# Final LayerNorm of a decoder layer: scaling on ACT and bias by accumulating transfers, last block on VectorE

## Chip, core and metric

The kernel runs on one core of one Trainium2 chip. The metric is device time in microseconds of one execution, the median of several runs; lower is better.

## The reference, cut to what matters

One decoder layer runs over a prompt of 512 rows and over 32 sample rows (8 sequences of 4), 2048 columns wide, in float32. The change lies in its last step, the output product with its residual and the LayerNorm behind it:

```python
def _layernorm(x, w, b):
    xf = x.astype(jnp.float32)
    mu = jnp.mean(xf, axis=-1, keepdims=True)
    var = jnp.mean(jnp.square(xf - mu), axis=-1, keepdims=True)
    return (xf - mu) * lax.rsqrt(var + LN_EPS) * w.astype(jnp.float32) + b.astype(jnp.float32)
...
    out = jnp.einsum('btc,cd->btd', y, w_out)
    return _layernorm(DN_ALPHA * x + out, ln_w, ln_b).astype(x.dtype)
```

The rest of the layer (the input projection, an mLSTM branch, a sliding-window attention branch and their gated merge) is the same before and after.

## The kernel before

The whole program is written out by Python loops. A list scheduler then orders each engine's instructions by a simulated timeline, among the ready ones by their place in the program; `tc.issue_after(x)` holds a block's instructions behind instruction `x` on its engine. Each engine works through its list in order and waits on semaphores. VectorE is DVE in the profile, TensorE is PE, GpSimd is POOL; SP issues the plain transfers, POOL the accumulating ones.

Most of the program is float32 products made of three products of split operands. The output product `y · w_out` runs over 16 column tiles of 128. Tiles 0 to 12 give transposed results: each is copied out of the accumulator by ACT and turned back by TensorE in `add_residual`, where VectorE adds `ALPHA * x`. The sums stand in one buffer, `z`, of 128 partitions by 4 blocks by 2048 columns; block t holds rows 128t to 128t + 127 of the prompt. The 32 sample rows lie folded into `zs`, 128 partitions by 512. `stats` gathers the LayerNorm statistics of each 512 columns as they come. In `residual_task`, `scaled(1, ...)` multiplies block 1 by `ln_w` in advance.

The last three column tiles (`G3 = 3`) are made transposed only for blocks 2 and 3 and the samples. For blocks 0 and 1 `rows_of(0)` and `rows_of(1)` make them as plain rows, the last large products of the program; each of these calls slips other work in behind its second step (`meanwhile`). So the order at the end is: the first two steps of `rows_of(0)`; the last residual of blocks 2, 3 and the samples, their `moments` and their `finish`; the rest of `rows_of(0)`; the first steps of `rows_of(1)`; block 0's residual, moments and `finish`; the rest of `rows_of(1)`; block 1.

`moments` makes mean and variance on VectorE and the power −1/2 on POOL (L1621), into the columns `m` and `r_` of `mv`. `finish` normalises a block in two halves of 1024 columns with two VectorE operations each: `(z - m) * lw` (L1635) and `z * r_ + lb` (L1640), and then stores each half to `y_p`. For the samples (t = 4) they are L1626 and L1627, with `lwq` and `lbq`. Block 0's second operation and its stores are put off (`later=True`, `rest0`) until block 1's statistics are through; `add_rows(1)`, block 1's residual and moments, is held behind block 0's first operations.

Block 1 ends in `finish_last`. As it is already multiplied by `lw`, what is left is `z * r_ + (lb - m * r_ * lw)`. The bracket is made by TensorE: `mr` holds `-m * r_` and a one for each row, is turned into two rows (`mrT`), and a product with the two rows `ln_w`, `ln_b` (`lrows`) gives 512 columns at a time (L1656). VectorE adds (L1657) and SP stores 256 KB (L1658), four times.

Elsewhere in the kernel POOL already issues accumulating transfers, which add one 512 KB buffer to another of the same shape (L617), and ACT already scales by a column of its own for each partition (L762).

Of the kernel before, what the change touches and what calls it, by code (L numbers as in the profile page):

```python
# [15 lines left out]
F32 = mybir.dt.float32  # L16
F32R = mybir.dt.float32r
AF = mybir.ActivationFunctionType
ALU = mybir.AluOpType

D = 2048
# [15 lines left out]
EPS = 1e-5  # L37
# [36 lines left out]
def _build(tc, nc, i, o, es):  # L74
# [3 lines left out]
    def pool(stack, name, bufs, space=None, side=None):  # L78
        kw = {"space": space} if space is not None else {}
        if space is None:  # L80
            kw["side"] = side or "right"
            kw["reuse_waits"] = "tile"
        return stack.enter_context(tc.tile_pool(name=name, bufs=bufs, **kw))

    y_p, y_s, C_p, n_p, m_p, kb_p, vb_p, C_s, n_s, m_s, kb_s, vb_s = o
    V, A, G, PE = nc.vector, nc.scalar, nc.gpsimd, nc.tensor
# [13 lines left out]
    def nm(s):  # L100
        count[0] += 1
        return f"{s}_{count[0]}"

    def sm():
        return psB.tile([128, 512], F32, tag="sm", name=nm("sm"))

    def ev(n=T):
        return evp.tile([128, n], F32, tag="ev", name=nm("ev"))
# [16 lines left out]
    state = {}  # L125
# [10 lines left out]
    def drain():  # L136
        while live:
            tick()
# [4 lines left out]
    ident = cc[:, C_ID:C_ID + 128]  # L143
# [161 lines left out]
    for g in range(8):  # L305
        for q in range(2):
            k = g * 2 + q
            pt = sm()
# [9 lines left out]
            else:  # L318
                hilo(pt[:], xk2[0][k // 4 - 2][:, k % 4, 0:SEQ], xk2[1][k // 4 - 2][:, k % 4, 0:SEQ])
                c = (slice(None), k - 8, slice(0, SEQ - HT))  # L320
                V.tensor_tensor(out=s1r[c], in0=pt[:, HT:SEQ], in1=s1r[c], op=ALU.subtract)
        if g % 2:
# [7 lines left out]
            else:  # L330
                hilo(src, *(xk2[p][g // 2 - 2][:, :, SEQ:T] for p in range(2)))
                c = (slice(None), slice(k4.start - 8, k4.stop - 8), slice(SEQ - HT, HT))
# [930 lines left out]
    def branch(src, p, tmp, ahead=()):  # L1263

        hs, los = act_tiles(p, "bh"), act_tiles(p, "bl")

        def steps():
            for k in range(KT):
                if k < len(ahead):
                    st = ahead[k]  # L1270
                else:
                    st = tmp(k)
                    nc.sync.dma_start(st[:], src[k])
                hilo(st[:], hs[k // 4][:, k % 4], los[k // 4][:, k % 4])
                yield
        return (hs, los), whole(hs), whole(los), steps()

    _, bah, bal, g_ = branch(d_bra, act, lambda k: ev(), ahead)
# [264 lines left out]
    d1 = pool(esD, "d1", 1)  # L1543
    z = d1.tile([128, 4, D], F32, name="z")
    lw = d1.tile([128, D], F32, name="lw")
    lb = d1.tile([128, D], F32, name="lb")
    zs = d1.tile([128, 512], F32, name="zs")[:]
    stt = d1.tile([128, 5, 4, 6], F32, name="stt")
    mv = d1.tile([128, 5, 4], F32, name="mv")
# [7 lines left out]
        nc.sync.dma_start(z[:, :, cs], xrows[:, :, cs])  # L1557
        nc.sync.dma_start(zs[r], xs_src[:, cs])

    mr = d1.tile([128, 2], F32, name="mr")  # L1560
    V.memset(mr[:], 1.0)

    def load_ln():
        nc.sync.dma_start(lw[:], i["ln_w"].partition_broadcast(128))
        nc.sync.dma_start(lb[:], i["ln_b"].partition_broadcast(128))
# [20 lines left out]
    def stats(lo, hi, c4):  # L1586
        for t in range(lo, min(hi, 4)):
            V.bn_stats(stt[:, t, c4], z[:, t, c4 * 512:c4 * 512 + 512])

    def scaled(t, c4):  # L1590
        c = slice(c4 * 512, c4 * 512 + 512)
        V.tensor_tensor(out=z[:, t, c], in0=z[:, t, c], in1=lw[:, c], op=ALU.mult)

    def evac(ot, ps, parts=(0, 1)):
        for f, c, w in CUT:
            if f in parts:
                A.copy(ot[:, c:c + w], ps[f][:, :w])

    def residual_task(ct, ot):
        add_residual(ct, ot, 0, 5)  # L1600
        if ct % 4 == 3:
            yield
            stats(0, 4, ct // 4)
            yield
            scaled(1, ct // 4)

    def moments(t):
        m = mv[:, t]
        if t < 4:
            V.bn_aggr(m[:, 0:2], stt[:, t])  # L1610
            state["moment"] = V.tensor_scalar(m[:, 1:2], m[:, 1:2], EPS, None, op0=ALU.add)
        else:
            V.bn_stats(stt[:, t, 0], zs)
            V.bn_aggr(m[:, 0:2], stt[:, t, 0:1])
            V.scalar_tensor_tensor(m[:, 1:2], m[:, 0:1], m[:, 0:1], m[:, 1:2], op0=ALU.mult, op1=ALU.add)
            pm = sm()
            PE.matmul(pm[:, 0:2], cq, m[:, 0:2], start=True, stop=True)
            V.tensor_copy(m[:, 0:2], pm[:, 0:2])
            V.scalar_tensor_tensor(m[:, 3:4], m[:, 0:1], m[:, 0:1], m[:, 1:2], op0=ALU.mult, op1=ALU.subtract)
            V.tensor_scalar(m[:, 1:2], m[:, 3:4], -1.0, EPS, op0=ALU.mult, op1=ALU.add)  # L1620
        G.tensor_tensor(out=m[:, 2:3], in0=m[:, 1:2], in1=mh[:, 0:1], op=ALU.pow)  # L1621

    def finish(t, later=False):
        m, r_ = mv[:, t, 0:1], mv[:, t, 2:3]
        if t == 4:
            V.scalar_tensor_tensor(zs, zs, m, lwq, op0=ALU.subtract, op1=ALU.mult)  # L1626
            V.scalar_tensor_tensor(zs, zs, r_, lbq, op0=ALU.mult, op1=ALU.add)  # L1627
            for q in range(4):
                nc.sync.dma_start(ys_rows[:, q * 512:q * 512 + 512], zs[q * 32:q * 32 + 32])
            return  # L1630
        dst = y_p[0, t * 128:t * 128 + 128, :]
        cs = [slice(c0, c0 + 1024) for c0 in range(0, D, 1024)]
        for c in cs:
            zt = z[:, t, c]
            state["scaled"] = V.scalar_tensor_tensor(zt, zt, m, lw[:, c], op0=ALU.subtract, op1=ALU.mult)  # L1635

        def rest():
            for c in cs:
                zt = z[:, t, c]
                V.scalar_tensor_tensor(zt, zt, r_, lb[:, c], op0=ALU.mult, op1=ALU.add)  # L1640
                nc.sync.dma_start(dst[:, c], zt)
        if later:
            return rest
        rest()

    def finish_last(t):

        m, r_ = mv[:, t, 0:1], mv[:, t, 2:3]
        V.scalar_tensor_tensor(mr[:, 0:1], m, -1.0, r_, op0=ALU.mult, op1=ALU.mult)
        pt = sm()  # L1650
        PE.transpose(pt[:2, 0:128], mr[:], ident)
        A.copy(mrT, pt[:2, 0:128])
        for q in range(4):
            c = slice(q * 512, q * 512 + 512)
            pc = sm()
            PE.matmul(pc[:], mrT, lrows[q // 2][:2, (q % 2) * 512:(q % 2) * 512 + 512], start=True, stop=True)  # L1656
            V.scalar_tensor_tensor(z[:, t, c], z[:, t, c], r_, pc[:], op0=ALU.mult, op1=ALU.add)  # L1657
            nc.sync.dma_start(y_p[0, t * 128:t * 128 + 128, c], z[:, t, c])  # L1658

    def tail_task(ct, ot):  # L1660
        add_residual(ct, ot, 2, 5)
# [2 lines left out]
    def add_rows(t):  # L1664

        cs = slice(D - G3 * 128, D)
        V.scalar_tensor_tensor(z[:, t, cs], z[:, t, cs], ALPHA, rows[t][:, 0:G3 * 128], op0=ALU.mult, op1=ALU.add)
        stats(t, t + 1, 3)
        moments(t)
# [3 lines left out]
    def rows_of(t, meanwhile):  # L1673
        ps = rows[t] = sm()
        for k in range(KT):
            if k == 2:
                meanwhile()
            yk = slice(t * 128, t * 128 + 128)
            hi, lo = yh_[k // 4][:, k % 4, yk], yl_[k // 4][:, k % 4, yk]
            for n, (a, p) in enumerate(((hi, 0), (hi, 1), (lo, 0))):  # L1680
                PE.matmul(ps[:, 0:G3 * 128], a, w3[k // 8][p][:, k % 8].rearrange("p g c -> p (g c)"),
                          start=(k == 0 and n == 0), stop=(k == KT - 1 and n == 2))
# [14 lines left out]
    for g in range(G3):  # L1697
        ct = 16 - G3 + g
        ps = sm()
        for half in range(2):  # L1700
            raw = load_half(wo, ct * 128, half)
            wh, wl = (w[:, :, g] for w in w3[half])
# [7 lines left out]
    def room(tag):  # L1710
        return wp.tile([128, 8, 128], F32, tag=tag, name=nm("room"))[:].rearrange("p a b -> p (a b)")

    lq, cm = room("wh"), room("wh")
    lwq, lbq, cq, mrT = lq[:, 0:512], lq[:, 512:1024], cm[:, 0:128], cm[:2, 128:256]
    nc.sync.dma_start(cq, i["consts"][:, C_Q:C_Q + 128])
    for q in range(4):
        r, cs = slice(q * 32, q * 32 + 32), slice(q * 512, q * 512 + 512)
        nc.sync.dma_start(lwq[r], i["ln_w"][cs].partition_broadcast(32))
        nc.sync.dma_start(lbq[r], i["ln_b"][cs].partition_broadcast(32))
    lrows = [room("wl") for _ in range(2)]  # L1720
    for h in range(2):
        for n, name in enumerate(("ln_w", "ln_b")):
            nc.sync.dma_start(lrows[h][n:n + 1], i[name][h * 1024:h * 1024 + 1024].unsqueeze(0))
    rows_of(0, lambda: (add_residual(15, ot, 2, 5), stats(2, 4, 3), [moments(t) for t in (2, 3, 4)], finish(2), finish(3), finish(4)))
    rest0 = []
    rows_of(1, lambda: (add_rows(0), rest0.append(finish(0, later=True))))
    with tc.issue_after(state["scaled"].ins):
        add_rows(1)
    with tc.issue_after(state["moment"].ins):
        rest0[0]()  # L1730
        scaled(1, 3)
    finish_last(1)
    drain()
    esD.close()

# [27 lines left out]
```

## Time and profile before

| | us |
|---|---|
| median of 3 runs (2523.73 to 2529.15) | 2525.47 |
| the profiled execution, its time | 2526.54 |
| its span, first to last instruction | 2524.8 |
| mean granted clock of TensorE | 0.994 |

Times in the profile count from the start of the span. Busy time of an engine is the sum of its instructions; a row of the timeline gives start, duration, engine, line, operation, what it writes and reads, the shape, how many were merged, and in brackets the idle time before it and what ended that. A row of the transfers gives packets, megabytes and the time that the packets took as a share of 16 DMA engines over the window asked for. A time to landing is counted from the issue of a transfer.

### The profile page before, as it was taken

How to read it: one execution, taken by the hardware profiler on the slowest of the kernel's cores; microseconds unless marked ns; L12 is line 12 of the kernel's file. 1: busy time of each engine (PE TensorE's matmuls, PEld its weight loads, DVE VectorE, ACT ScalarE, POOL GpSimd, SP SyncE). 2: the span in 40 equal slices, each digit the busy share in tenths (PEclk: the TensorE clock that was granted, in tenths of full speed). 3: DMA queues.
4: the chain of work that ended last, by engine and by line, in shares of the span. 5: the costliest groups of instructions: out<-in, count | busy, mean ns of one | idle time of the engine just before them, and what ended most of it. 6: DMA issues, size and time to landing. Idle time of an engine off the chain costs nothing.

```text
span 2524.8 us, 48516 instructions
## 1 busy us (share of the span) xinstructions
PE 2496.1 (99%) x19667; PEld 2430.7 (96%) x19667; DVE 1765.6 (70%) x2690; ACT 1210.3 (48%) x1966; POOL 364.6 (14%) x347
## 2 busy tenths in 40 slices
PE   8999999999999999999999999999999999999997
PEld 8999999999999999999999999999999999999996
DVE  8867777677677677777777877777856655764335
ACT  4457676676676664443433544434633333433220
POOL 0111211211211211122111222111000000110000
PEclk8999999999999999999999999999999999999998
DMA  6776666666666654577577577576755556888232
GB/s 167 169 188 160 152 151 160 152 149 162 152 148 163 152 143 116 129 219 221 165 226 223 156 215 219 170 225 199 231 176 173 184 170 208 217 218 268 84 108 82
DMA packets 544505, 439.86 MB, mean 174 GB/s; under 512 B 44084, under 2 KB 451556, under 8 KB 543992
## 3 DMA queue, kind: packets, MB, share of 16 engines
q1 hardware_dynamic: 531320, 389.30, 52.1%
q0 software_dynamic: 12960, 47.45, 9.9%
q8 instruction: 154, 2.52, 0.4%
q14 instruction: 71, 0.58, 0.1%
HBM read 305.76 MB, written 90.04 MB: 157 GB/s over the span
## 4 chain that ended last, share of the span: by engine, by line
PE 52%; issue 4%; DVE 1%; DMA 1%; POOL 0%; ACT 0%; POOLq 0%; DVEq 0%
PE bank L639 20%; PE bank L204 12%; PE bank L641 10%; PE sm L1334 2%; PE sm L1153 1%; PE sm L1147 1%; PE sm L1366 1%; PE sm L1379 1%; PE sm L204 1%; DMA tx<-d_brm 1%; PE sm L1656 0%; PE sm L1313 0%; PE sm L1321 0%; PE sm L1575 0%; DVE z L1640 0%
## 5 line engine op out<-in xcount | busy, mean ns | idle before, releaser
L195 ACT CAST wh<-raw 128x1024 fp32r<-128x1024 f32 x620 | 649.2, 1048 | 860.1 <-PE bank L639 620.5
L196 DVE TENSOR_TENSOR wl<-raw,wh 128x1024 fp32r<-128x1024 f32 x620 | 764.1, 1233 | 294.4 <-ACT wh L195 254.3
L639 PE MATMUL bank<-xk,wh 128*128 128x272 f32 x2336 | 321.8, 288 | 0.6 <-DVE ev L664 0.6
L639 PEld LDWEIGHTS bank<-xk,wh 128*128 128x128 f32 x2336 | 303.6, 188 | 4.2 <-ACT wh L195 1.7
L619 DVE TENSOR_TENSOR raw<-raw,raw 128x1024 f32<-128x1024 f32 x230 | 292.2, 1272 | 10.2 <-DMA raw<-in_w_in 5.5
L658 POOL TENSOR_TENSOR ev<-p,ev 128x272 f32<-128x272 f32 x78 | 117.7, 1509 | 570.1 <-ACT ev L657 515.9
L641 PE MATMUL bank<-xk,wl 128*128 128x272 f32 x1168 | 173.5, 288 | 0.0
L639 PE MATMUL bank<-n2h,wh 128*128 128x272 f32 x624 | 160.6, 288 | 2.1 <-ACT wh L195 2.1
L639 PE MATMUL bank<-s1h,wh 128*128 128x272 f32 x624 | 161.9, 290 | 0.7 <-ACT wh L195 0.7
L639 PE MATMUL bank<-n3l,wh 128*128 128x272 f32 x624 | 161.4, 290 | 0.0
L639 PE MATMUL bank<-s4h,wh 128*128 128x272 f32 x624 | 161.1, 289 | 0.1
L639 PE MATMUL bank<-n3h,wh 128*128 128x272 f32 x624 | 161.1, 289 | 0.0
L639 PE MATMUL bank<-n2l,wh 128*128 128x272 f32 x624 | 160.8, 290 | 0.0
L639 PE MATMUL bank<-s1l,wh 128*128 128x272 f32 x624 | 160.7, 290 | 0.0
L639 PE MATMUL bank<-s4l,wh 128*128 128x272 f32 x624 | 160.4, 290 | 0.0
L641 PEld LDWEIGHTS bank<-xk,wl 128*128 128x128 f32 x1168 | 156.7, 188 | 0.1
L639 PE MATMUL bank<-a11l,wh 128*128 128x272 f32 x584 | 150.1, 290 | 0.0
L639 PE MATMUL bank<-a11h,wh 128*128 128x272 f32 x584 | 149.9, 288 | 0.0
L204 PE MATMUL bank<-bh,wl 128*128 128x272 f32 x704 | 148.1, 289 | 0.0
L204 PE MATMUL bank<-bh,wh 128*128 128x272 f32 x704 | 147.8, 290 | 0.0
L204 PE MATMUL bank<-bl,wh 128*128 128x272 f32 x704 | 147.2, 288 | 0.0
L639 PEld LDWEIGHTS bank<-n2h,wh 128*128 128x128 f32 x624 | 117.2, 188 | 2.5 <-ACT wh L195 2.3
(443 smaller groups left out, 5619.0 us busy)
## 6 DMA issues: line engine op xcount, KB each, us to landing
raw<-in_w_in SPq DMA_DIRECT2D x296, 512.0 KB, 4.7
raw<-raw POOLq DMA_DIRECT2D x82, 512.0 KB, 4.9
C<-in_state_mlstm_C SPq DMA_DIRECT2D x32, 1024.0 KB, 6.3
out<-C SPq DMA_DIRECT2D x64, 512.0 KB, 3.8
raw<-in_w_proj_a SPq DMA_DIRECT2D x32, 512.0 KB, 4.8
raw<-in_w_proj_m SPq DMA_DIRECT2D x32, 512.0 KB, 5.5
raw<-in_w_out SPq DMA_DIRECT2D x32, 512.0 KB, 4.1
d_sgm<-ev SPq DMA_DIRECT2D x16, 272.0 KB, 4.1
```

Source lines behind the costliest of these rows:

```text
L195: A.copy(wh[:, k:k + n], raw[:, k:k + n])
L196: V.tensor_tensor(out=wl[:, k:k + n], in0=raw[:, k:k + n], in1=r32(wh[:, k:k + n]), op=ALU.subtract)
L204: PE.matmul(ps[f][:, :w], a[:, kk], b(k, c, w), start=(k == 0 and n == 0), stop=(k == 15 and n == 2))
L619: V.tensor_tensor(out=w[out][:], in0=w[a][:], in1=w[b][:], op=ALU.add)
L639: PE.matmul(ps, wh[:, k], x(p, k), start=(first and k == 0 and p == 0), stop=False, skip_group_check=True)
L641: state["end"] = PE.matmul(ps, wl[:, k], x(0, k), start=False, stop=(k == 7), skip_group_check=True)
L658: G.tensor_tensor(out=c22, in0=p1, in1=c11, op=ALU.subtract)
L1147: PE.matmul(pC[c * 32:c * 32 + 32, :], qz[:, c], ct[:, c], start=(b == 0), stop=(b == NB - 1), tile_position=(0, c * 32))
L1153: PE.matmul(pu[:], Ab[:, c * 128:c * 128 + 128], r["V4"][:], start=True, stop=True)
L1334: PE.matmul(pp[:, 0:258], a[:, b * 128:b * 128 + 128], b_[:, b, f], start=(b == 0 and n == 0), stop=(b == 3 and n == 2))
L1366: PE.matmul(pp[:, 0:n], x_[c][:, b * 128:b * 128 + 128], y_[c][:, b * 128:SEQ], start=(c == 0 and m == 0), stop=(c == 3 and m == 2))
L1379: PE.matmul(pp[:, 0:258], x_[:, off:off + 128], y_[:, b, f], start=(b == 0 and n == 0), stop=(b == j and n == 2))
```

## The change

Every block but block 1 still has `(z - m) * lw` on VectorE, but ACT then multiplies by `r_`, and POOL issues a transfer from `lb` into `z` that adds what it brings to what is there. SP's store of that half follows it. The samples go the same way with `lbq`, in one piece. `finish(t, n, both)` takes the width of a piece and the column from which VectorE does the second operation itself; block 1 is called with 512 and 0, so it has eight VectorE operations of 512 columns: first four subtractions with weights, then four with scale and bias, each followed by its store.

Block 1 is no longer multiplied by `lw` in advance (`scaled` goes); `finish_last`, `mr`, `mrT`, `lrows` with their four loads, the small products and the two `issue_after` holds go, and block 0's `finish` is no longer put off.

```diff
-    mr = d1.tile([128, 2], F32, name="mr")
-    V.memset(mr[:], 1.0)
...
-    def scaled(t, c4):
-        c = slice(c4 * 512, c4 * 512 + 512)
-        V.tensor_tensor(out=z[:, t, c], in0=z[:, t, c], in1=lw[:, c], op=ALU.mult)
...
             stats(0, 4, ct // 4)
-            yield
-            scaled(1, ct // 4)
...
-    def finish(t, later=False):
+    def finish(t, n=1024, both=D):
+
         m, r_ = mv[:, t, 0:1], mv[:, t, 2:3]
         if t == 4:
             V.scalar_tensor_tensor(zs, zs, m, lwq, op0=ALU.subtract, op1=ALU.mult)
-            V.scalar_tensor_tensor(zs, zs, r_, lbq, op0=ALU.mult, op1=ALU.add)
+            A.activation(zs, zs, AF.Copy, scale=r_)
+            G.dma_start(out=zs, in_=lbq, accum_op=ALU.add)
...
         dst = y_p[0, t * 128:t * 128 + 128, :]
-        cs = [slice(c0, c0 + 1024) for c0 in range(0, D, 1024)]
+        cs = [slice(c0, c0 + n) for c0 in range(0, D, n)]
         for c in cs:
             zt = z[:, t, c]
-            state["scaled"] = V.scalar_tensor_tensor(zt, zt, m, lw[:, c], op0=ALU.subtract, op1=ALU.mult)
-
-        def rest():
-            for c in cs:
-                zt = z[:, t, c]
+            V.scalar_tensor_tensor(zt, zt, m, lw[:, c], op0=ALU.subtract, op1=ALU.mult)
+            if c.start < both:
+                A.activation(zt, zt, AF.Copy, scale=r_)
+                G.dma_start(out=zt, in_=lb[:, c], accum_op=ALU.add)
+        for c in cs:
+            zt = z[:, t, c]
+            if c.start >= both:
                 V.scalar_tensor_tensor(zt, zt, r_, lb[:, c], op0=ALU.mult, op1=ALU.add)
-                nc.sync.dma_start(dst[:, c], zt)
-        if later:
-            return rest
-        rest()
-
-    def finish_last(t):
...
+            nc.sync.dma_start(dst[:, c], zt)
...
-    rest0 = []
-    rows_of(1, lambda: (add_rows(0), rest0.append(finish(0, later=True))))
-    with tc.issue_after(state["scaled"].ins):
-        add_rows(1)
-    with tc.issue_after(state["moment"].ins):
-        rest0[0]()
-        scaled(1, 3)
-    finish_last(1)
+    rows_of(1, lambda: (add_rows(0), finish(0)))
+    add_rows(1)
+    finish(1, 512, 0)
```

More of the change, by code (lines that the diff above doesn't have):

```diff
@@ L1610, in moments @@
             V.bn_aggr(m[:, 0:2], stt[:, t])
-            state["moment"] = V.tensor_scalar(m[:, 1:2], m[:, 1:2], EPS, None, op0=ALU.add)
+            V.tensor_scalar(m[:, 1:2], m[:, 1:2], EPS, None, op0=ALU.add)
         else:
@@ L1631, in finish @@
         dst = y_p[0, t * 128:t * 128 + 128, :]
-        cs = [slice(c0, c0 + 1024) for c0 in range(0, D, 1024)]
+        cs = [slice(c0, c0 + n) for c0 in range(0, D, n)]
         for c in cs:
             zt = z[:, t, c]
-            state["scaled"] = V.scalar_tensor_tensor(zt, zt, m, lw[:, c], op0=ALU.subtract, op1=ALU.mult)
-        def rest():
-            for c in cs:
-                zt = z[:, t, c]
-                V.scalar_tensor_tensor(zt, zt, r_, lb[:, c], op0=ALU.mult, op1=ALU.add)
-                nc.sync.dma_start(dst[:, c], zt)
-        if later:
-            return rest
-        rest()
-    def finish_last(t):
[L1648 to L1658, printed above, removed]
+            V.scalar_tensor_tensor(zt, zt, m, lw[:, c], op0=ALU.subtract, op1=ALU.mult)
[5 more added lines that the diff above has]
+            if c.start >= both:
+                V.scalar_tensor_tensor(zt, zt, r_, lb[:, c], op0=ALU.mult, op1=ALU.add)
+            nc.sync.dma_start(dst[:, c], zt)
     def tail_task(ct, ot):
@@ L1713, in _build @@
     lq, cm = room("wh"), room("wh")
-    lwq, lbq, cq, mrT = lq[:, 0:512], lq[:, 512:1024], cm[:, 0:128], cm[:2, 128:256]
+    lwq, lbq, cq = lq[:, 0:512], lq[:, 512:1024], cm[:, 0:128]
     nc.sync.dma_start(cq, i["consts"][:, C_Q:C_Q + 128])
@@ L1719, in _build @@
         nc.sync.dma_start(lbq[r], i["ln_b"][cs].partition_broadcast(32))
[L1720 to L1723, printed above, removed]
     rows_of(0, lambda: (add_residual(15, ot, 2, 5), stats(2, 4, 3), [moments(t) for t in (2, 3, 4)], finish(2), finish(3), finish(4)))
-    rest0 = []
-    rows_of(1, lambda: (add_rows(0), rest0.append(finish(0, later=True))))
-    with tc.issue_after(state["scaled"].ins):
-        add_rows(1)
-    with tc.issue_after(state["moment"].ins):
-        rest0[0]()
-        scaled(1, 3)
-    finish_last(1)
+    rows_of(1, lambda: (add_rows(0), finish(0)))
+    add_rows(1)
+    finish(1, 512, 0)
     drain()
```

## Prediction

> **What bounds the kernel now.** I read the page first, then the timeline of the last 35 us engine by engine, then the transfers of that stretch. The page:
>
> ```profile
> PE 2496.1 (99%) x19667; PEld 2430.7 (96%) x19667; DVE 1765.6 (70%) x2690; ACT 1210.3 (48%) x1966; POOL 364.6 (14%) x347
> q1 hardware_dynamic: 531320, 389.30, 52.1%
> q0 software_dynamic: 12960, 47.45, 9.9%
> ```
>
> TensorE is busy for 99% of the span, so up to its last product nothing that the change touches is on the path: the three multiplications by `lw` that it takes out of the output product lie under matmuls. All of its effect must lie behind that product, in the last 22 us of 2524.8. The timeline there (start, duration, engine, line):
>
> ```profile
> 2502.71 0.34 PE L1681 MATMUL sm<-w,yl 128*128 128x384 f32 x1
> 2492.59 1.28 DVE L1635 SCALAR_TENSOR_TENSOR z<-z,mv,lw 128x1024 f32<-128x1024 f32 x1
> 2493.98 3.67 DVE L1635 SCALAR_TENSOR_TENSOR z<-z,mv,lw 128x1024 f32<-128x1024 f32 x3
> 2497.57 1.27 DVE L1640 SCALAR_TENSOR_TENSOR z<-z,mv,lb 128x1024 f32<-128x1024 f32 x1
> 2498.76 0.54 DVE L1667 SCALAR_TENSOR_TENSOR z<-z,sm 128x384 f32<-128x384 f32 x1
> 2499.30 3.66 DVE L1640 SCALAR_TENSOR_TENSOR z<-z,mv,lb 128x1024 f32<-128x1024 f32 x3
> 2502.88 0.68 DVE L1588 BATCH_NORM_STATS2 stt<-z 128x6 f32<-128x512 f32 x1
> 2503.61 0.74 DVE L1626 SCALAR_TENSOR_TENSOR zs<-zs,mv,room 128x512 f32<-128x512 f32 x1
> 2507.01 0.55 DVE L1667 SCALAR_TENSOR_TENSOR z<-z,sm 128x384 f32<-128x384 f32 x1
> 2509.16 0.15 DVE L1611 TENSOR_SCALAR mv<-mv 128x1 f32<-128x1 f32 x1
> 2512.22 0.15 DVE L1649 SCALAR_TENSOR_TENSOR mr<-mv 128x1 f32<-128x1 f32 x1
> 2513.14 7.19 PE L1656 MATMUL sm<-room,room 2*128 2x512 f32 x8 [0.34 <-ACT room L1652]
> 2520.37 0.75 DVE L1657 SCALAR_TENSOR_TENSOR z<-z,mv,sm 128x512 f32<-128x512 f32 x1 [0.96 <-PE sm L1656]
> 2516.03 5.45 SPq L1658 DMA_DIRECT2D out<-z  x4
> ```
>
> The last product ends at 2503.05. VectorE is then behind: it still works off the four bias operations of blocks 2 and 3 (L1640), so block 1's residual (second L1667) comes only at 2507.01. From there the end runs through block 1: moments to 2509.31, `mr` at 2512.22, four pairs of small float32 products (7.19 us), the last addition to 2521.12, its store. The path is VectorE, then TensorE; the transfers wait for them.
>
> **What goes.** VectorE loses six L1640 of 1.27 us, the last `zs` operation (0.74), the scaling of block 1 and `mr`; TensorE loses the 7.19 us. Block 1 gets eight operations of 512 columns, 8 × 0.74 = 5.9 us at most. In the new order VectorE has, from 2492.6, four L1635 (to 2497.65), block 0's residual, statistics and moments, the four samples' operation and two more L1635: 0.5 + 0.7 + 0.5 + 0.7 + 2.5 = 4.9 us, to about 2502.6, before the last product. Block 1's residual starts at 2503.2, its moments are there at about 2504.9 (2.3 us in the rows above, from 2507.01 to 2509.31, less a `zs` operation of 0.74 that ran between them), and its eight operations end at 2510.8, 10.3 us sooner than 2521.12. Were VectorE the end, that would be the gain. I do not think it is.
>
> **What comes: ACT and the POOL issues.** Prices from these rows (ACT's own 1024-column copy, its two sizes of scaling by a column, the kernel's accumulating transfer, the power of the variance):
>
> ```profile
> L195 ACT CAST wh<-raw 128x1024 fp32r<-128x1024 f32 x620 | 649.2, 1048 | 860.1 <-PE bank L639 620.5 <-PE bank L204 157.1 <-DVE c L1494 13.6
> L762 ACT ACTIVATE s<-s,sums 128x256 f32<-128x256 f32 x96 | 41.5, 495 | 0.0
> L762 ACT ACTIVATE s<-s,sums 128x128 f32<-128x128 f32 x32 | 12.8, 399 | 4.9 <-DVE sums L759 4.9
> 2492.82 2.85 POOL L1621 TENSOR_TENSOR mv<-mv,mh 128x1 f32<-128x1 f32 x2 [238.41 <-DVE mv L1611]
> 94.44 0.87 POOL L617 DMA_DIRECT2D raw<-raw  x1 [0.36 <-issue]
> ```
>
> 495 − 399 ns for 128 columns gives 0.75 ns a column, so 1024 columns cost 0.495 + 768 × 0.00075 = 1.07 us on an otherwise idle ACT. The first chunk of block 2 leaves VectorE at 2493.87, needs the first power (half of the 2.85 us: about 2494.3), leaves ACT at 2495.4; POOL is free of the second power at 2495.67 and issues the first accumulation then. The other six follow as VectorE delivers, at 0.87 us an issue: the last, of block 0, at about 2504. Block 1's power queues behind it on POOL until about 2506.5, which VectorE's four subtractions (to about 2507.8) cover.
>
> **What comes: the accumulating transfers.** One such transfer of 512 KB alone, in the 6 us from 94.4 (40 slices of 0.15 us):
>
> ```profile
> DMA  0000000007909194959899590911000000000297
> q0 software_dynamic: 144, 0.52, 46.1%
> raw<-raw POOLq DMA_DIRECT2D x1, 512.0 KB, 4.5
> ```
>
> It is issued at 94.44; its packets run from slice 9, about 1.4 us later, and hold all 16 DMA engines for 0.461 × 6 = 2.77 us; with completion it lands after 4.5. Over the whole run the page's 9.9% is 250 us; less eight plain loads on that queue (1.46 us each, by the row of two under the rivals) it is 2.9 us for each of 82. The plain transfers of the tail, in the 31 us from 2495, and the last four stores, in the 9 us from 2516 (slices of 0.225):
>
> ```profile
> q1 hardware_dynamic: 1632, 4.46, 36.7%
> DMA  0001997000059930000999000039950000000000
> q1 hardware_dynamic: 576, 1.05, 30.1%
> ```
>
> 0.367 × 31 = 11.4 us of all engines for every output store from 2495 on, which the change keeps. The last four take 0.301 × 9 / 4 = 0.68 each, and from the last one's end (slice 29, about 2522.8) to the end of the span are 2.0 us: completion and closing.
>
> **The Trainium skill**, "DMA: Bandwidth & Descriptors", section "Anatomy of one DMA — SWDGE (gpsimd) path", gives a POOL transfer about 2.0 us plus its bytes at 436 GB/s: an estimate of 3.2 us for 512 KB, 1.2 of it data. The trace does not agree: 4.5 at least, 2.77 of it on the engines. What a plain rate would make of the end is the second rival.
>
> **The sum.** Six accumulations of 512 KB and one of 256 KB: 6 × 2.77 + 1.45 = 18.1 us. The small one has no row (packets half as long); it costs between half a large one (1.4) and a whole one (2.77), and I take 1.45, since the last stores (0.68) show cost going nearly with bytes. With the stores 18.1 + 11.4 = 29.5 us of work for the same 16 engines. It starts at 2495.7 + 1.4 = 2497.1, and the backlog does not run dry: by 2505.4, when the last accumulation's packets could first start, only 8.3 of the 29.5 are done. SP issues in order, so block 1's stores, ready from about 2508.5, stand behind block 0's, which wait for its accumulations; issued ahead they would only take their turn earlier. Near the end there is an idle stretch: from the last accumulation's end to the packets of the store behind it lie 0.33 us (4.5 − 1.4 − 2.77) and the store's issue, about 0.85 (VectorE's end at 2521.12 to late in slice 26); the store before it fills some 0.7 of that, 0.5 is left.
>
> 2497.1 + 29.5 + 0.5 + 2.0 = 2529.1, against 2524.8: 4.3 us longer. The 10 us that VectorE and TensorE give up are taken by a queue of transfers that now ends last. The profiled execution took 2526.54 with its 2524.8 span; the median of the three runs is 2525.47, 1.07 below it. So 2525.47 + 4.3 = **2529.8**. About 0.2%, 5.05 us, is what a measurement here can tell: the border lies at 2530.5.
>
> Bounds: the small accumulation adds up to 1.3; 2.9 instead of 2.77 for each adds 0.9; the idle stretch is 0 to 1.2; an ACT or POOL step up to 0.5 sooner or later at the start; and the runs lie from 2523.73 to 2529.15. That is 2526 to 2533 in this case. Removed, at nothing: `mr`'s memset and four 4 KB loads under the matmuls; their cover is 99% TensorE, and without it they would be below 1 us.
>
> **Rivals.** *One at a time* (slower). Seven transfers have never stood on POOL's queue together in this trace. If each accumulation begins only once the one before has landed, the queue paces the end: 2495.7 + 6 × 4.9 (median landing) + 3.6 (half the data less) = 2528.7, then block 0's last store 0.85 + 1.28, block 1's 2.7, closing 2.0: 2535.5, 10.7 us longer, 2536.2. It decides as soon as a landing, and not the 2.77 us on the engines, separates two of them.
>
> ```profile
> L617 POOL DMA_DIRECT2D raw<-raw x82: 832/858/1007, 54.8 to 2253.6; - x82
> DMA to landing us min/median/max: 4.5/4.9/13.6
> 2125.80 1.46 POOL L1474 DMA_DIRECT2D tx<-d_brm  x2 [78.29 <-DVE s4l L238]
> q0 software_dynamic: 288, 1.11, 29.2%
> tx<-d_brm POOLq DMA_DIRECT2D x2, 544.0 KB, 6.5
> ```
>
> The last three rows, from the 10 us after 2125, speak against it: two plain loads issued 0.73 us apart landed 6.5 us after issue, and both together took 2.9 us of the engines, so two stood in the queue at once. Chance 0.09.
>
> *Plain rate* (faster). If queued accumulations moved like those loads and stores, 1.28 us for 512 KB, the work is 6.5 × 1.28 + 11.4 = 19.7 and the end 2497.1 + 19.7 + 2.0 = 2518.8, 6 us shorter: 2519.5. For it speaks that none was seen with another right behind it; against it that the 2.77 us are filled by 144 packets, nine in a row on each engine. This is what the skill's formula amounts to. Chance 0.05. Shorter still, by VectorE's 10 us, it could be only if the transfers cost nothing; I give that nothing.
>
> **How the numbers follow.** The queue of transfers as summed has 0.86, its centre 0.8 us below the border of slower and its unknown terms mostly upward: 0.47 within 0.2%, 0.39 above. With the first rival's 0.09, slower is 0.48; faster 0.05 is the second. The range 2526 to 2535 holds the main case and the approach to the first rival.
>
> **What would show it.** Right: no L1656; VectorE's last operation near 2510; DMA busy at nine tenths from 2497 to about 2526 with q0 near 18 us; each store's issue waiting on an accumulation; `z<-lb` landing far above 4.9 us (queueing). Wrong: gaps in the DMA row between accumulations (first rival), packets of an accumulation taking 1.3 us (second), a last store waiting for VectorE, or TensorE's last product not at 2503.

## Result, and the profile after

The changed kernel takes 2530.01 us (median of 20 runs, 2527.01 to 2534.8) against 2525.22 in the same session: 4.8 us between the medians. The ratio is 1.0018, with an interval of 1.0011 to 1.0025. So the changed kernel is longer; whether by more than 0.2%, the interval leaves open. Its profiled execution has a span of 2528.6 us, against 2524.8.

Up to the last large product the two profiles differ little: it ends at 2502.92, before at 2503.05. From the page (engines, then DMA queues):

```profile
PE 2487.6 (98%) x19658; PEld 2425.9 (96%) x19658; DVE 1758.3 (70%) x2681; ACT 1217.7 (48%) x1972; POOL 370.6 (15%) x354
q1 hardware_dynamic: 531312, 389.29, 51.7%
q0 software_dynamic: 13968, 50.86, 10.6%
```

The timeline of the end, engine by engine:

```profile
2502.58 0.34 PE L1659 MATMUL sm<-w,yl 128*128 128x384 f32 x1
2493.91 3.67 DVE L1628 SCALAR_TENSOR_TENSOR z<-z,mv,lw 128x1024 f32<-128x1024 f32 x3
2499.84 2.47 DVE L1628 SCALAR_TENSOR_TENSOR z<-z,mv,lw 128x1024 f32<-128x1024 f32 x2
2502.96 0.56 DVE L1645 SCALAR_TENSOR_TENSOR z<-z,sm 128x384 f32<-128x384 f32 x1 [0.65 <-PE sm L1659]
2507.29 2.73 DVE L1635 SCALAR_TENSOR_TENSOR z<-z,mv,lb 128x512 f32<-128x512 f32 x4
2494.27 4.51 ACT L1630 ACTIVATE z<-z,mv 128x1024 f32<-128x1024 f32 x4 [8.27 <-POOL mv L1612]
2495.72 0.88 POOL L1631 DMA_DIRECT2D z<-lb  x1
2505.22 0.85 POOL L1631 DMA_DIRECT2D z<-lb  x1 [0.18 <-issue]
2500.40 11.54 SPq L1636 DMA_DIRECT2D out<-z  x5
2512.96 4.10 SPq L1622 DMA_DIRECT2D out<-zs  x4
2517.16 6.82 SPq L1636 DMA_DIRECT2D out<-z  x5
```

VectorE now waits 0.65 us for the last large product, where before it was behind that product, and is done with everything at 2510.02; before, it was done at 2521.12. Yet the span is longer. Five stages of the end, with busy time of each engine and the share of the DMA engines:

```profile
core 0: us, PE busy (x) PEld busy (x) DVE busy (x) ACT busy (x) POOL busy (x), PEclk, DMA share, GB/s
2489.00:2497.00 8.00, 8.00 (x49) 7.80 (x48) 7.33 (x15) 2.71 (x3) 3.97 (x4) 1.00 0.00 0
2497.00:2503.00 6.00, 5.92 (x34) 5.60 (x33) 5.33 (x12) 2.77 (x4) 5.40 (x6) 1.00 1.04 194
2503.00:2510.00 7.00, 0.00 (x0) 0.00 (x0) 6.90 (x12) 1.92 (x2) 3.30 (x4) 0.75 1.04 248
2510.00:2520.00 10.00, 0.00 (x0) 0.00 (x0) 0.03 (x1) 0.00 (x0) 0.00 (x0) 0.50 1.06 275
2520.00:2529.00 9.00, 0.00 (x0) 0.00 (x0) 0.00 (x0) 0.00 (x0) 0.00 (x0) 0.50 0.73 247
```

From 2510 on the compute engines do next to nothing (0.03 us on VectorE); the DMA engines are full until about 2527. A share above 1 is no error: packet times are summed, and they overlap a little. The transfers from 2495 to 2530 (slices of 0.875 us), and who SP waited for (us in total, times, longest; the wait of 30.8 us began long before this stretch):

```profile
DMA  0079999999999999899999999999999999971000
GB/s 0 0 140 192 192 178 197 201 201 197 215 253 267 257 272 243 269 307 288 279 290 290 243 276 272 267 295 208 288 141 300 363 405 407 412 309 75 0 9 0
q0 software_dynamic: 1008, 3.41, 51.6%
q1 hardware_dynamic: 1632, 4.46, 35.8%
z<-lb POOLq DMA_DIRECT2D x6, 512.0 KB, 9.7
out<-z SPq DMA_DIRECT2D x6, 512.0 KB, 4.2
SPq L1636 <- DMA z<-lb: 39.4, 4, 30.8
```

No gap stands in the DMA row from 2497 to 2527. While accumulations have the engines alone they move 178 to 201 GB/s; at the end, from 2523 to 2525.6 with only stores left, it is 405 to 412.

### The profile page after: what moved, and what is told of

It reads as the page before. It is cut to its first block, busy times and chain, and to the rows that moved or that the text cites. A ratio compares the mean times of both kernels' runs of the same rounds, so it can differ in the third digit from the quotient of the medians.

```text
span 2528.6 us, 48504 instructions
## 1 busy us (share of the span) xinstructions
PE 2487.6 (98%) x19658; PEld 2425.9 (96%) x19658; DVE 1758.3 (70%) x2681; ACT 1217.7 (48%) x1972; POOL 370.6 (15%) x354
## 4 chain that ended last, share of the span: by engine, by line
PE 90%; issue 4%; DVE 2%; DMA 2%; ACT 0%; POOL 0%; SPq 0%; DVEq 0%; POOLq 0%; ACTq 0%
PE bank L639 42%; PE bank L641 21%; PE bank L204 13%; PE sm L1334 2%; PE sm L1153 1%; PE sm L1147 1%; PE sm L1366 1%; PE sm L745 1%; PE sm L1379 1%; PE sm L783 1%; PE sm L773 1%; PE sm L204 1%; PE sm L1659 1%; DMA tx<-d_brm 1%; DVE wl L196 0%
```

## The experiments

The last product ends at different times in the profiled executions (2500.33 to 2505.62). The shift is older than the part that was changed: in the stretch from about 2350 to 2493, the same 1100 matmuls take 139.6 to 139.7 us in all nine profiles. A part of it goes with the clock: between 2163 and 2171 the mean granted clock was 0.79 in the changed kernel, e3 and e6 and 1.00 in the other six, and the 500 matmuls around that time took 66.5 to 66.8 us in the three and 64.2 to 65.1 in the six. What made the rest is open.

So spans are compared by the *tail*, from the end of that product to the end of the span. Before it is 2524.8 − 2503.05 = 21.75 us, after 2528.6 − 2502.92 = 25.7. Each tail is of one profile, and the time from the last packet to the end of the span is itself 1.4 us in some and 2.0 in others, so less than a microsecond between two tails says nothing. The ratios, from 9 to 20 runs each, give the same order, but for e1 and e4, whose tails lie 0.3 us apart.

| kernel | accumulations | last product ends | span | tail | ratio to before, interval |
|---|---|---|---|---|---|
| before | 0 | 2503.05 | 2524.8 | 21.75 | |
| changed | 7 | 2502.92 | 2528.6 | 25.7 | 1.0018, 1.0011 to 1.0025 |
| e1 | 0 (7 copies) | 2502.96 | 2519.5 | 16.5 | 0.9979, 0.9970 to 0.9989 |
| e2 | 7 of an eighth | 2504.97 | 2518.3 | 13.3 | one run only |
| e3 | 7 | 2505.62 | 2530.5 | 24.9 | 1.0014, 1.0004 to 1.0023 |
| e4 | 0 | 2500.33 | 2517.1 | 16.8 | 0.9976, 0.9966 to 0.9986 |
| e5 | 2 | 2502.93 | 2517.6 | 14.7 | 0.9974, 0.9965 to 0.9983 |
| e6 | 4 | 2500.85 | 2519.0 | 18.15 | 0.9982, 0.9973 to 0.9991 |
| e7 | 5 (4 and the samples') | 2500.80 | 2520.5 | 19.7 | 0.9994, 0.9985 to 1.0003 |

The last products of the seven kernels, e1 to e7 in order:

```profile
2502.62 0.34 PE L1659 MATMUL sm<-w,yl 128*128 128x384 f32 x1
2504.63 0.34 PE L1659 MATMUL sm<-w,yl 128*128 128x384 f32 x1
2505.28 0.34 PE L1683 MATMUL sm<-w,yl 128*128 128x384 f32 x1
2499.99 0.34 PE L1658 MATMUL sm<-w,yl 128*128 128x384 f32 x1
2502.59 0.34 PE L1658 MATMUL sm<-w,yl 128*128 128x384 f32 x1
2500.51 0.34 PE L1658 MATMUL sm<-w,yl 128*128 128x384 f32 x1
2500.46 0.34 PE L1659 MATMUL sm<-w,yl 128*128 128x384 f32 x1
```

**e1: the same transfers, copying instead of adding.**

```diff
-                G.dma_start(out=zt, in_=lb[:, c], accum_op=ALU.add)
+                G.dma_start(out=zt, in_=lb[:, c])
...
-            G.dma_start(out=zs, in_=lbq, accum_op=ALU.add)
+            G.dma_start(out=zs, in_=lbq)
```

> The changed kernel with its seven POOL transfers as plain copies of the same size (they overwrite instead of adding, so the bias replaces the normalised values). Theory A, the 16 DMA engines' work on accumulations sets the end: the copies cost 1.28 us instead of 2.77 for 512 KB, 6.5 x 1.28 + 12 = 20.3 us of work from 2497.2, closing 2.0: span near 2519.5, 9 us below the changed kernel's 2528.6. Rival B, the number of POOL transfers and their passage through ACT, POOL and SP sets it: span stays within 1 us of 2528.6. Rival C, VectorE's and TensorE's path through block 1 sets it: stays too.

Measured: span 2519.5, ratio 0.9979. POOL's queue over the 40 us from 2490, after and in e1:

```profile
q0 software_dynamic: 1008, 3.41, 45.2%
q0 software_dynamic: 944, 3.41, 21.6%
```

The same 3.41 MB cost 18.1 us of all 16 engines as accumulations and 8.6 us as copies, 2.8 against 1.3 us for 512 KB. The tail is 9.1 us shorter, though the stations are nearly the same: VectorE ends at 2510.05 (2510.02 with accumulations), and the last POOL issue comes at 2503.99 instead of 2505.22, since POOL's issues too are shorter for a copy, about 0.54 us against 0.85. Neither the number of POOL transfers nor VectorE's path explains 9 us. Why adding takes twice as long as copying, the runs do not show.

**e2: the accumulations cut to an eighth.**

```diff
-                G.dma_start(out=zt, in_=lb[:, c], accum_op=ALU.add)
+                G.dma_start(out=z[:, t, c.start:c.start + 128], in_=lb[:, c.start:c.start + 128], accum_op=ALU.add)
...
-            G.dma_start(out=zs, in_=lbq, accum_op=ALU.add)
+            G.dma_start(out=zs[:, 0:64], in_=lbq[:, 0:64], accum_op=ALU.add)
```

> The changed kernel with each accumulation cut to an eighth of its columns (128 of 1024, 64 of 512; the other columns get no bias). Theory A: the engines' work falls by some 15 us, the queue runs dry, and the end comes from VectorE's last operation near 2510 and the stores behind it, which SP issues in order: span 2514 to 2517. Rival B (fixed costs of each transfer, not its bytes): all seven are still there, span within 2 us of 2528.6. Rival C: 2528.6.

```profile
DMA  0000000005599999988759999930000000000000
q0 software_dynamic: 1008, 0.43, 9.8%
2509.35 2.73 DVE L1635 SCALAR_TENSOR_TENSOR z<-z,mv,lb 128x512 f32<-128x512 f32 x4
```

All seven transfers are there, but the queue takes 3.9 us in place of 18 (more than an eighth, so not all of the cost goes with bytes). The span of 2518.3 is above the 2514 to 2517 expected, because the last product came 2.05 us later than in the changed kernel; by the tail it would be 2516.2. This is a single run. It ends 6.2 us behind VectorE's last operation (2512.08), because the stores themselves fill the engines in the meantime. A fixed cost for each transfer is not what binds in the changed kernel.

**e3: the accumulations alone, block 1 as before.**

```diff
             V.scalar_tensor_tensor(zs, zs, m, lwq, op0=ALU.subtract, op1=ALU.mult)
-            V.scalar_tensor_tensor(zs, zs, r_, lbq, op0=ALU.mult, op1=ALU.add)
+            A.activation(zs, zs, AF.Copy, scale=r_)
+            G.dma_start(out=zs, in_=lbq, accum_op=ALU.add)
...
             state["scaled"] = V.scalar_tensor_tensor(zt, zt, m, lw[:, c], op0=ALU.subtract, op1=ALU.mult)
+            A.activation(zt, zt, AF.Copy, scale=r_)
+            G.dma_start(out=zt, in_=lb[:, c], accum_op=ALU.add)
...
-                V.scalar_tensor_tensor(zt, zt, r_, lb[:, c], op0=ALU.mult, op1=ALU.add)
                 nc.sync.dma_start(dst[:, c], zt)
```

> The kernel before with only the scaling on ACT and the accumulating transfers taken over; block 1 still ends in its small products on TensorE. Theory A: block 1's form is off the path, span 2528 to 2530, time equal to the changed kernel's within 1 us, some 4 us above before. Rival C: block 1's longer way (12 us from its moments to its last addition, against 5.5) shows: span near 2535.

```profile
2517.46 0.75 DVE L1659 SCALAR_TENSOR_TENSOR z<-z,mv,sm 128x512 f32<-128x512 f32 x1 [0.96 <-PE sm L1658]
DMA  0000000003999999999999999999999999999600
```

The small products on TensorE are back and VectorE is busy until 2518.21, 12.6 us behind the last product instead of 7.1. It costs nothing: the tail is 24.9 against 25.7, the ratio 1.0014 against 1.0018, their intervals overlapping. SP's stores come in another order here, three of block 1's between the two of block 0, and that does not show either. While the accumulations are there, block 1's form does not matter.

**e4: no accumulation at all.** Every block finishes on VectorE; only the second part of the change is left.

```diff
-            A.activation(zs, zs, AF.Copy, scale=r_)
-            G.dma_start(out=zs, in_=lbq, accum_op=ALU.add)
+            V.scalar_tensor_tensor(zs, zs, r_, lbq, op0=ALU.mult, op1=ALU.add)
...
-    rows_of(0, lambda: (..., finish(2), finish(3), finish(4)))
-    rows_of(1, lambda: (add_rows(0), finish(0)))
+    rows_of(0, lambda: (..., finish(2, 1024, 0), finish(3, 1024, 0), finish(4)))
+    rows_of(1, lambda: (add_rows(0), finish(0, 1024, 0)))
```

> The changed kernel without any accumulating transfer: all blocks and the samples finish on VectorE, block 1 as in the changed kernel. Theory A: the transfers no longer bind; VectorE gets back 6 x 1.22 + 0.66 us less an idle 0.65, ends near 2517, and the end of the span is 3.7 us behind it: 2521, 4 us below before and 7.5 below the changed kernel. If the change's second part (block 1 on VectorE) were itself the loss, it would stay above before's 2524.8.

```profile
2511.18 2.73 DVE L1634 SCALAR_TENSOR_TENSOR z<-z,mv,lb 128x512 f32<-128x512 f32 x4
DMA  0000000959996000056994199500000000000000
```

The DMA row has gaps again and the end follows VectorE, which ends at 2513.91; the span ends 3.2 us behind it. Ratio 0.9976, and the tail is 5.0 us shorter than before. So the two parts of the change have opposite signs: block 1 on VectorE, with the order that goes with it, is worth about 5 us by the tail, and the accumulations cost more than that, 8.9 us between the tails of e4 and of the changed kernel. The end came earlier than expected: of the 3.9 us below the 2521 expected, 2.6 are the earlier last product, and 1.3 that VectorE lost less than summed and the end lay closer behind it.

**e5, e6, e7: two, four and five accumulations.** e5 keeps them for block 2 alone, e6 for blocks 2 and 3, e7 for these and the samples; the rest finishes on VectorE, by the same edits as in e4.

> The changed kernel with accumulations for block 2 alone; blocks 3 and 0 and the samples finish on VectorE. Theory A: engine work 2 x 2.77 + 12 = 17.5 us from 2497.2, not binding; VectorE ends near 2514.8 (the changed kernel's 2510 with 4 x 1.22 + 0.66 us more, less 0.65 idle), span 3.7 us behind it, 2518.5: 6 us below before, 10 below the changed kernel. Rival B (each transfer's fixed passage): two seventh of the way back from the changed kernel, no lower than without accumulations (2521).

> Accumulations for blocks 2 and 3, the rest on VectorE. Theory A: the engines bind again: 4 x 2.77 + 12 = 23.1 us from 2497.2, closing 2.0, span 2522.3, though VectorE ends sooner (2512.4) than with two accumulations. Were VectorE the end, it would be 2516.

> The changed kernel with block 0 alone taken off the accumulations (blocks 2, 3 and the samples keep them). Theory A: 5.5 us of engine work less, span 2523 to 2524. Rival C (VectorE's path): VectorE gets 2 x 1.22 us more ahead of block 1, span 2530.5.

POOL's and SP's queues over 40 us, then VectorE's last operations, of e5, e6 and e7 in order; for e6 also the DMA row (slices of 1 us):

```profile
q1 hardware_dynamic: 1632, 4.46, 28.9%
q0 software_dynamic: 288, 1.05, 13.9%
2511.73 2.73 DVE L1634 SCALAR_TENSOR_TENSOR z<-z,mv,lb 128x512 f32<-128x512 f32 x4
...
q1 hardware_dynamic: 1632, 4.46, 29.6%
q0 software_dynamic: 576, 2.10, 27.6%
DMA  0000099999999999999999999990000000000000
2507.32 2.73 DVE L1634 SCALAR_TENSOR_TENSOR z<-z,mv,lb 128x512 f32<-128x512 f32 x4
...
q0 software_dynamic: 720, 2.36, 31.4%
q1 hardware_dynamic: 1632, 4.46, 30.0%
2507.12 2.73 DVE L1635 SCALAR_TENSOR_TENSOR z<-z,mv,lb 128x512 f32<-128x512 f32 x4
```

POOL's queue takes 5.6, 11.0 and 12.6 us: 2.8 for each large accumulation, 1.5 for the samples'. With two (e5) VectorE still sets the end, at 2514.46, 3.1 us ahead of it; its tail of 14.7 is the shortest of the kernels that compute the whole result, 2.1 below that of e4, which has none. With four (e6) VectorE is done at 2510.05 and the end comes 9 us later, behind a DMA row without a gap from 2495 to 2517: the engines bind. A fifth, the samples', adds 1.55 us of tail for 1.5 us of engine work; block 0's two, from e7 to the changed kernel, add 6.0 us for 5.5. From two to four the tail grows though VectorE has less to do. Counted to the last product of the changed kernel, e5, e6 and e7 end at 2517.6, 2521.1 and 2522.6, where 2518.5, 2522.3 and 2523 to 2524 were expected; the sums were about 1 us too long in each.

e5 is below both kernels of the study, at 0.9974 of before, some 6.6 us. Against e4 it is not apart: their intervals overlap, and they were timed in different sessions on different chips. That two accumulations are better than none therefore rests on one tail of each, and is not shown.

## Why the prediction was right

The forecast was 2529.8 for 2530.01 measured, and a span of 2529.1 for 2528.6. The mechanism was the one forecast. That the times agree to 0.2 us is luck: the spans of the two profiles differ by 3.8 us, the medians by 4.8, and the interval of the ratio is some 3.5 us wide. Step by step:

- VectorE's end, 10.3 us sooner: it ended at 2510.02 (2510.8 forecast), block 1's residual starting at 2502.96 (2503.2). That this gain would not show is the main claim, and e3 and e4 show it: with accumulations block 1's form is worth nothing, without them it is worth 5 us.
- The first accumulation: issued at 2495.72 (2495.7 forecast). ACT took 1.15 us for 1024 columns, the median of six (1.07). The last issue was at 2505.22, not 2504, since both powers and the samples' transfer stood ahead of it on POOL; the backlog covered that, as the prediction had it for any late issue.
- The work of accumulating: 0.516 × 35 = 18.06 us, forecast 18.1. The part without a row, the samples', is 12.56 − 11.04 = 1.5 between e7 and e6, forecast 1.45.
- The stores were mis-sized: 0.358 × 35 = 12.5 us, not 11.4. In e4 and e5, where they run mostly without other transfers, they take 11.5 to 11.6; in e3, with the same seven accumulations, 11.8; in e1, beside copies, 11.9. Other transfers alongside lengthen them, then, but what makes it 12.5 here is open.
- Against that, the counted work passes in less time than its sum, since packet times overlap. This is so with accumulations alone: in the first row below, of the 3 us from 2497, their queue has 105.1% of 16 engines. So 30.6 us of counted work fit into the 30.0 from 2497.1 to the last packet near 2527.1, and the 0.5 us idle stretch was not seen as a gap. The sum's 29.5 + 0.5 = 30.0 is right only because these errors cancel.
- The closing was mis-sized: from the last packets (second row, the 2.6 us from 2526 in slices of 0.065) to the end of the span are 1.4 us, not 2.0. This is the half microsecond by which the span was forecast too long.

```profile
q0 software_dynamic: 159, 0.59, 105.1%
DMA  3939146190333303000000000000000000000000
```

- One accumulation at a time, the slower rival: none of it. The DMA row has no gap, and while they wait for each other a median of 9.7 us passes to landing.
- The plain rate, the faster rival: 2518.8 was worked out for it, and e1, which makes it true, ended at 2519.5. The rival's price was about right (1.3 us measured for 512 KB, 1.28 forecast), and its condition was not met. The Trainium skill, "DMA: Bandwidth & Descriptors", section "Anatomy of one DMA — SWDGE (gpsimd) path", puts the data at bytes over 436 GB/s, an estimate of 1.2 us for 512 KB. The copies of e1 took 1.3 us of the engines, the accumulations 2.8: that part of the formula comes near for copying here, and not for adding.

## What to carry to other kernels

Work moved from an engine to a transfer is not free because the engine is: sum what the DMA engines then have to carry in that stage, stores included, and see which sum ends last. An accumulating transfer of 512 KB took the DMA engines 2.1 times as long as a copy of the same bytes here, so look for a stretch in which they are idle: two accumulations found room in it and did not set the end, four and seven did. And a change of two parts can hide the gain of one behind the loss of the other; take them apart before judging either.

## What was not expected of the hardware

A store issued while accumulations were queued did not share the engines with them at once: SP issued the first at 2500.40, and the rate in the GB/s row stays at the accumulations' 197 to 201 until about 2503.7; up to then the profile has no packet of SP's queue. In e4, with nothing ahead of it, the first store is issued at 2496.22 and its packets come 0.9 us later. SP's issues also grew longer: the samples' four stores took 1204 ns in the median, against 413 before:

```profile
L1622 SPq DMA_DIRECT2D out<-zs x4: 330/1204/1219, 2513.0 to 2515.8; - x4
L1629 SPq DMA_DIRECT2D out<-zs x4: 330/413/425, 2508.2 to 2509.6; - x4
```

They took about as long in e3, e6 and e7 (1186 to 1216 ns), but 420 in e5, where the DMA row is full at that time too, with stores alone. So full engines are not enough for it, and what is remains open.

And where the last large product ends varied by 5 us between profiled executions of programs that are nearly the same up to there, more than the effect under study. Where only one profile of a kernel is at hand, the tail tells more than the span.
